# Three modulation steps a unit in the first MLP's second half, and the gate multiplied into three weight tiles of the second MLP

## Chip, core and metric

The kernel runs on one core of a Trainium2 chip. The core has five engines that run side by side, each through its own instructions in order: TensorE (PE) for matmuls, VectorE (DVE), ScalarE (ACT), GpSimd (POOL), and SyncE (SP), which here only issues DMAs. Weights come from HBM by DMA. The metric is the device time of one execution in microseconds (us).

## What is computed

Two transformer layers with adaptive modulation over 256 latent tokens (t = 0, 1 of 128 tokens each) and, in the first layer only, 256 context tokens (t = 2, 3). Layer 0 mixes by retention, layer 1 by neighbourhood attention; each is followed by an MLP. The parts that matter here:

```python
mod = (silu_c @ ada_w[i] + ada_b[i])[:, None, :]
sh1, sc1, g1, sh2, sc2, g2 = jnp.split(mod, 6, axis=-1)
...
x = layer_norm(DN_ALPHA * x + g1 * y, ln_g[i, 0], ln_b[i, 0])
h = x * (1.0 + sc2) + sh2
x = layer_norm(DN_ALPHA * x + g2 * sq_relu_mlp(h, mlp_w1[i], mlp_w2[i]), ln_g[i, 1], ln_b[i, 1])
```

`sq_relu_mlp` is `square(relu(h @ w1)) @ w2` with 4096 hidden columns. The gate g2 is one number per output column, the same for all tokens, so `g2 * (r @ w2)` is `r @ (w2 * g2)`.

## The kernel before

**Precision.** Every float32 operand is split into a high half (`hi`, a rounded cast by ACT) and a low half (`lo = raw - hi`, by DVE), and each product is three matmuls (hi*hi, hi*lo, lo*hi; `mm3`). So each weight tile goes through a fixed path: a DMA of 512 KB into a `raw` buffer (SP), a cast to `hi` (ACT), a subtraction to `lo` (DVE), then matmuls. `raw` has four buffers, `hi` and `lo` five each. `specs` lists all weight tiles in the order of use; `take` and `fetch` (L250 on) bring them in, `take` up to five ahead.

**Modulation as background work.** The products with `ada_w` that layer 1 needs are made bit by bit beside the matmuls. `bg(n)` (L556) does n steps; a step loads one 512 KB slice of `ada_w` (`rawa`, into the same four raw buffers and by the same SP queue) and has DVE weigh the slice before it into an accumulator (`acc<-rawa`). Each eight slices end in a fold (`red<-acc`) and some small work. There are 89 steps (`bg_max`); 41 are done before the first MLP, 16 in the second layer of its first half.

**First MLP (layer 0).** The hidden columns are done in two halves (`hf`). A half has eight units of the first layer (two weight tiles, 48 matmuls of 512 columns, then a squared relu into `hid` by ACT and DVE), and then the second layer over two halves of the output columns, each with eight weight tiles (24 matmuls each) into four PSUM banks. In the half with hf = 1, `bg(2 + fp % 2)` (L1332) does two and three steps by turns after each unit, 20 in all, and `bg()` (L1357) one after each of the next twelve weight tiles; with that the 89 are done. The last four weight tiles of the last half are held (`held = take(4)`): they are multiplied token tile by token tile, so that the normalization of one tile can run beside the matmuls of the next, and all four are needed within the first token tile's 24 matmuls.

**Second MLP (layer 1).** Only latent tokens. Its second layer has 16 units u of 256 weight rows, each in two halves of the output columns; `parts` holds four PSUM accumulators (token tile t, half). The last three units (HELD = 13 on) are held and done in the order (t 0, half 0), (t 0, half 1), (t 1, half 0), (t 1, half 1), the last of these in two quarters of the columns that have PSUM banks of their own. `settle` multiplies an accumulator by the gate (`gated`, DVE, out of PSUM) and adds it to the residual R; `settle_quarter` does it for a quarter; `stat` and `moments` make the mean and variance, `last_norm` the output. From the held units on, PE, ACT, DVE and POOL keep the order of the program text. Nearly all instructions are recorded in one helper (`InOrder`, L84), so the profile's rows all carry L84, and tiles tell them apart.

In the order of the held part, `settle(1, 1)`, for the finished units of (t 1, half 1), stands between the two halves of token tile 0.

Of the kernel before, what the change touches and what calls it, by code (L numbers as in the profile page):

```python
# [17 lines left out]
P = 128  # L18
# [86 lines left out]
def kernel(  # L105
# [23 lines left out]
    pe, act, dve, pool, sp = (  # L129
        InOrder(tc, getattr(nc, e), e in PIN)  # L130
        for e in ("tensor", "scalar", "vector", "gpsimd", "sync")
    )
# [23 lines left out]
    def bank(s="ps"):  # L156
        return psp.tile([P, 512], F32, tag="ps", name=nm(s))
# [5 lines left out]
    def scr(s, dt=F32):  # L163
        return scp.tile([P, 512], dt, tag="scr", name=nm(s))
# [18 lines left out]
    specs = []  # L183
# [54 lines left out]
    def spec_w2(u, half):  # L238
        w_rows(mlp_w2[1], u * 256, 256, half * 512, 512)


    scratch_units = set()
    for u in range(16):
        for half in range(2):
            if (u, half) == (10, 0):
                scratch_units.add(len(specs))
                spec_w2(13, 0)
            if (u, half) != (13, 0):
                spec_w2(u, half)

    units = []
# [3 lines left out]
    def fetch(n, in_scratch=False, at=None):  # L255

        for src, k, ncol in specs[len(units) : len(units) + max(n, 0)]:
            raw = rawp.tile([P, k, ncol], F32, tag="raw", name=nm("raw"))
            sp.dma_start(out=raw[:], in_=src.rearrange("(k p) n -> p k n", p=P))
            if in_scratch or len(units) in scratch_units:  # L260
                hi, lo = Rows([scr("hi", F32R) for _ in range(k)]), Rows([scr("lo", F32R) for _ in range(k)])
                for i in range(k):
                    act.copy(out=hi[:, i, :], in_=raw[:, i, :])
                    pending.append((lo[:, i, :], raw[:, i, :], hi[:, i, :]))
                units.append((hi, lo))
                continue
            if at is None:
                hi = hip.tile([P, k, ncol], F32R, tag="hi", name=nm("hi"))
                lo = lop.tile([P, k, ncol], F32R, tag="lo", name=nm("lo"))
            else:  # L270
                both = slot(at, [P, 2, k, ncol], F32R, "hilo")
                hi, lo = both[:, 0], both[:, 1]
            act.copy(out=hi[:], in_=raw[:])
            pending.append((lo[:], raw[:], hi[:]))
            units.append((hi, lo))
# [99 lines left out]
    R = [RR[t // 2][:, t % 2, :] for t in range(4)]  # L375
# [180 lines left out]
    def bg(n=1):  # L556
        for _ in range(n):
            if bg_done[0] < bg_max[0]:
                flush()
                bg_done[0] += 1  # L560
                next(bgs, None)
# [5 lines left out]
    def load_gate(l, w, nt=2, eng=nc.scalar):  # L567
        G = cpool.tile([P, 2, D], F32, tag="G", name=nm("G"))
        gt = grow[l, w]
        for t in range(nt):  # L570
            eng.dma_start(out=G[:, t, :], in_=gt[t : t + 1, :].broadcast_to([P, D]))
        return G
# [83 lines left out]
    def stat(t, half):  # L656
        if half == 0:
            stats[t] = smp.tile([P, 2, 6], F32, tag="st", name=nm("st"))
        dve.bn_stats(out=stats[t][:, half, :], in_=R[t][:, half * 512 : (half + 1) * 512])
# [212 lines left out]
    def part_v(k, a, b):  # L872
# [8 lines left out]
        out=lgn[:, 0], in_=ret_decay[0].rearrange("(o d) h -> o (d h)", o=1).broadcast_to([P, 8])  # L881
# [118 lines left out]
    for h in range(RH):  # L1000
# [9 lines left out]
        else:  # L1010
# [15 lines left out]
            for u in range(4):  # L1026
                ((wh, wl),) = take(1)
                for t in range(4):
                    for kk in range(2):
                        k = 2 * u + kk  # L1030
# [72 lines left out]
        for t in range(4):  # L1103
            po = bank("po")
            scs = list(range(4)) if t < 2 else [2, 3]
            for i, sc in enumerate(scs):
# [9 lines left out]
                out=on, in0=po[:], scalar1=mv[:, 0:1], scalar2=r[:], op0=ALU.subtract, op1=ALU.mult  # L1116
# [51 lines left out]
        else:  # L1168
# [35 lines left out]
            tmp = proj(1, 1)  # L1204
# [10 lines left out]
            tmp = proj(2, 1)  # L1215
# [54 lines left out]

    G2 = None
    for hf in range(2):
# [46 lines left out]
        for fp in range(len(hid), 8):  # L1319
            ht = hslot(fp)  # L1320
            pb = [bank("p1") for _ in range(2)]
            us = take(2)
            mm1(us, ALL, pb)
            pe.on = False
            dve.on = hf == 0
            evac1(pb, ALL, ht)
            if hf == 0 and fp < 6:
                residual(fp - 2, xns[fp - 2], gb, dve)
            dve.on = False
            hid.append(ht)  # L1330
            if hf:
                bg(2 + fp % 2)  # L1332
            if hf == 0 and fp < 6:
                for q in range(16 * (fp - 2), 16 * (fp - 1)):
                    shifted_biases(q)
        if G2 is None:
            G2 = load_gate(0, 1)
        for half in range(2):
# [19 lines left out]
            if not last:  # L1358
                for t in range(4):
                    accumulate(pb[t], t, half, G2)  # L1360
                continue
            bg_until(89)
            held = take(4)
# [14 lines left out]
            def settle(t):  # L1378

                add_to(t, 1, gated(pb[t], t, 1, G2), dve)  # L1380
                stat(t, 1)
                return moments(t)
# [336 lines left out]
    p2 = turn(2)  # L1719
# [183 lines left out]
    ps = bank("pnw")  # L1903
# [93 lines left out]
    ps = [wo_last(1, 1, cols) for cols in HALVES]  # L1997
# [58 lines left out]


    G2 = load_gate(1, 1, 1)
    HS1 = [N_Q, N_V, N_B, N_P0, N_P1, N_OH, N_OL, N_K1]
    hid = [ht]  # L2060
    for f4 in range(1, 8):
# [22 lines left out]

    FULL = slice(0, 512)
    parts = {(t, half): [(bank("p2"), FULL)] for t in range(2) for half in range(2)}
    HELD = 13

    def mm2b(t, half, u, un, only=None):
        wh, wl = un  # L2090
        for i, (ps, cols) in enumerate(parts[t, half]):
            if only in (None, i):
                for kk in range(2):
                    k = 2 * u + kk
                    ht = hid[k // 4]
                    mm3(
                        ps[:, cols],
                        (ht[:, k % 4, 0, tsl(t)], ht[:, k % 4, 1, tsl(t)]),
                        (wh[:, kk, cols], wl[:, kk, cols]),
                        k == 0 or (len(parts[t, half]) > 1 and k == 2 * HELD),  # L2100
                        k == 31 or (t == half == 1 and k == 2 * HELD - 1),
                    )

    held = {}
    for u in range(HELD):
        if u == 10:
# [13 lines left out]
    def quarter(q):  # L2120
        return slice(256 * q, 256 * q + 256)
# [3 lines left out]

    def settle_quarter(q):
        ps = parts[1, q // 2][q % 2][0][:, quarter(q % 2)]
        tmp = scr("acc")
        dve.tensor_mul(out=tmp[:, :256], in0=ps, in1=G2[:, 0, quarter(q)])
        dve.tensor_add(out=R[1][:, quarter(q)], in0=R[1][:, quarter(q)], in1=tmp[:, :256])  # L2130
        stat_quarter(q)

    def stat_quarter(q):
# [14 lines left out]
        if a:  # L2148
            (sp, act)[half].dma_start(out=out[0, tsl(t), sl], in_=xn)

    for half in range(2):
        for u in range(13, 16):
            mm2b(0, half, u, held[u, half])
        if half == 0:
            settle(1, 1)
            parts[1, 1] = [(bank("p2"), slice(256 * q, 256 * q + 256)) for q in range(2)]
        settle(0, half)
        stat(0, half)
    m0 = moments(0)
    for half in range(2):  # L2160
        last_norm(0, 0, half, *m0)
# [51 lines left out]
```

## Time and profile before

| | us |
|---|---|
| median of 3 runs | 1177.96 (1176.31 to 1180.05) |
| the profiled execution | 1176.32 |
| its span, first to last instruction | 1174.4 |
| PE busy | 1161.8 |
| DVE busy | 848.4 |
| ACT busy | 481.1 |

Rows of the timeline give start, duration, engine, operation, output<-inputs and shape, and in brackets how long the engine had been idle and what ended it. "x2" puts equal neighbours in one row. Matmuls are pipelined, so a row's duration is longer than the distance to the next one's start; a PE gap is read from start to start. An SP row gives the time at which a DMA was issued. The granted TensorE clock was 0.998 of full speed on average.

### The profile page before, as it was taken

How to read it: one execution, taken by the hardware profiler on the slowest of the kernel's cores; microseconds unless marked ns; L12 is line 12 of the kernel's file. 1: busy time of each engine (PE TensorE's matmuls, PEld its weight loads, DVE VectorE, ACT ScalarE, POOL GpSimd, SP SyncE). 2: the span in 40 equal slices, each digit the busy share in tenths (PEclk: the TensorE clock that was granted, in tenths of full speed). 3: DMA queues.
4: the chain of work that ended last, by engine and by line, in shares of the span. 5: the costliest groups of instructions: out<-in, count | busy, mean ns of one | idle time of the engine just before them, and what ended most of it. 6: DMA issues, size and time to landing. Idle time of an engine off the chain costs nothing.

```text
span 1174.4 us, 17544 instructions
## 1 busy us (share of the span) xinstructions
PE 1161.8 (99%) x6687; PEld 980.7 (84%) x6687; DVE 848.4 (72%) x1361; ACT 481.1 (41%) x819; POOL 235.1 (20%) x418
## 2 busy tenths in 40 slices
PE   9999999999999999999999999999999999999997
PEld 6788888888888889888888888879778878999886
DVE  3786687777898787757777675578577589877456
ACT  3643332222323246441212333137466666756341
POOL 0102001010220241770312001223443430000001
PEclk9999999999999999999999999999999999999999
DMA  9943552544355426756556665646344335766760
GB/s 275 277 130 105 162 187 96 156 153 144 112 178 177 140 65 220 181 113 215 177 184 198 211 200 179 197 157 202 81 136 144 107 113 160 214 206 205 237 215 36
DMA packets 140115, 195.10 MB, mean 166 GB/s; under 512 B 9936, under 2 KB 81136, under 8 KB 140032
## 3 DMA queue, kind: packets, MB, share of 16 engines
q1 hardware_dynamic: 131904, 182.03, 49.8%
q0 software_dynamic: 6976, 9.39, 3.8%
q10 hardware_dynamic: 1152, 2.56, 0.7%
q8 instruction: 52, 0.85, 0.3%
q14 instruction: 31, 0.25, 0.1%
HBM read 189.12 MB, written 5.75 MB: 166 GB/s over the span
## 4 chain that ended last, share of the span: by engine, by line
PE 74%; DMA 12%; DVE 8%; issue 3%; ACT 2%; POOL 0%; DVEq 0%; ACTq 0%
PE p L84 23%; DMA rawa<-in_ada_w_dram 11%; PE pq L84 8%; PE pv L84 8%; PE pw L84 7%; PE pg L84 7%; PE pn L84 4%; DVE acc L84 4%; PE pnv L84 4%; PE po L84 3%; DVE lo L84 3%; PE pnw L84 1%; PE ppt L84 1%; PE pS L84 1%; PE pav L84 1%
## 5 line engine op out<-in xcount | busy, mean ns | idle before, releaser
L84 ACT CAST hi<-raw 128x1024 fp32r<-128x1024 f32 (+2 forms) x228 | 231.9, 1032 | 306.7 <-PE p L84 114.2
L84 DVE TENSOR_TENSOR lo<-raw,hi 128x1024 fp32r<-128x1024 f32 (+2 forms) x228 | 272.6, 1210 | 101.3 <-ACT hi L84 101.1
L84 PE MATMUL p<-hi,hid 128*128 128x512 f32 (+1 forms) x780 | 238.2, 386 | 0.0
L84 PEld LDWEIGHTS p<-hi,hid 128*128 128x128 f32 x780 | 145.7, 188 | 29.3
L84 PE MATMUL p<-hTl,hi 128*128 128x256 f32 (+1 forms) x512 | 165.9, 326 | 0.0
L84 PE MATMUL p<-hTh,lo 128*128 128x256 f32 (+1 forms) x512 | 165.9, 326 | 0.0
L84 PE MATMUL p<-hTh,hi 128*128 128x256 f32 (+1 forms) x512 | 162.6, 327 | 0.0
L84 PE MATMUL p<-lo,hid 128*128 128x512 f32 (+1 forms) x390 | 150.8, 387 | 2.1 <-DVE lo L84 2.1
L84 DVE SCALAR_TENSOR_TENSOR acc<-rawa,scol,acc 128x1024 f32<-128x1024 f32 x56 | 74.4, 1341 | 65.1 <-DMA rawa<-in_ada_w_dram 65.1
L84 PEld LDWEIGHTS p<-hTh,lo 128*128 128x128 f32 x512 | 96.3, 188 | 8.8
L84 PEld LDWEIGHTS p<-hTl,hi 128*128 128x128 f32 x512 | 96.4, 188 | 8.7
L84 PEld LDWEIGHTS p<-hTh,hi 128*128 128x128 f32 x512 | 94.3, 188 | 8.7
L84 PEld LDWEIGHTS p<-lo,hid 128*128 128x128 f32 x390 | 73.3, 188 | 17.9 <-DVE lo L84 3.2
L84 DVE SCALAR_TENSOR_TENSOR strips<-rawa,scol,strips 128x512 f32<-128x512 f32 x112 | 78.6, 764 | 0.0
L84 ACT CAST hid<-r 128x256 fp32r<-128x256 f32 (+1 forms) x64 | 31.9, 500 | 112.4 <-DVE r L84 112.3
L84 POOL TENSOR_TENSOR rstd<-rstd,misc 128x1 f32<-128x1 f32 x28 | 19.1, 684 | 216.5 <-DVE rstd L84 215.5
L84 ACT ACTIVATE s<-s,mn 128x512 f32<-128x512 f32 x64 | 45.5, 713 | 21.6 <-DVE mn L84 21.6
L84 PE MATMUL pw<-hi,oh 128*128 128x512 f32 x128 | 50.8, 397 | 0.0
L84 PE MATMUL pg<-hi,hTh 128*128 128x512 f32 x128 | 50.6, 395 | 0.0
L84 PE MATMUL pw<-hi,ol 128*128 128x512 f32 x128 | 50.0, 390 | 0.0
L84 PE MATMUL pg<-hi,hTl 128*128 128x512 f32 x128 | 49.9, 390 | 0.0
L84 PE MATMUL pw<-lo,oh 128*128 128x512 f32 x128 | 49.8, 389 | 0.0
(241 smaller groups left out, 2275.2 us busy)
## 6 DMA issues: line engine op xcount, KB each, us to landing
raw<-in_mlp_w_dram SPq DMA_DIRECT2D x128, 512.0 KB, 4.5
rawa<-in_ada_w_dram SPq DMA_DIRECT2D x80, 512.0 KB, 3.9
raw<-in_ret_w_in_dram SPq DMA_DIRECT2D x42, 512.0 KB, 4.0
raw<-in_nat_w_in_dram SPq DMA_DIRECT2D x24, 512.0 KB, 4.1
rawq<-in_ada_w_dram SPq DMA_DIRECT2D x16, 512.0 KB, 6.0
raw<-in_ret_w_o_dram SPq DMA_DIRECT2D x16, 512.0 KB, 3.5
bias<-rpb_rows POOLq DMA_DIRECT2D x32, 128.0 KB, 2.9
raw<-in_nat_w_o_dram SPq DMA_DIRECT2D x8, 512.0 KB, 3.7
```

The lines of the kernel that those rows point to most:

```text
L84: r = f(*args, **kwargs)
```

## The change

Three edits. First, `bg(2 + fp % 2)` becomes `bg(3)`: 24 steps instead of 20 in the eight units, so that the 89 are done four steps earlier and the last half of the second layer has none. Second, the tiles of units 13 to 15, half 1, of the second MLP's second layer are multiplied by the gate in place, between their DMA and their cast (three products of 128x2x512 by DVE). Third, what these tiles give for half 1 goes to banks of its own (one for token tile 0, two quarters for token tile 1, as before), is added to R without a further product, and the accumulators of units 0 to 12 of half 1 are settled with the gate for both token tiles after `settle(0, 0)`.

```diff
--- before.py
+++ after.py
@@ -239,13 +239,16 @@
         w_rows(mlp_w2[1], u * 256, 256, half * 512, 512)
 
 
-    scratch_units = set()
+    HELD = 13
+    scratch_units, scaled_units, scale_row = set(), set(), [None]
     for u in range(16):
         for half in range(2):
             if (u, half) == (10, 0):
                 scratch_units.add(len(specs))
                 spec_w2(13, 0)
             if (u, half) != (13, 0):
+                if half == 1 and u >= HELD:
+                    scaled_units.add(len(specs))
                 spec_w2(u, half)
 
     units = []
@@ -257,6 +260,10 @@
         for src, k, ncol in specs[len(units) : len(units) + max(n, 0)]:
             raw = rawp.tile([P, k, ncol], F32, tag="raw", name=nm("raw"))
             sp.dma_start(out=raw[:], in_=src.rearrange("(k p) n -> p k n", p=P))
+            if len(units) in scaled_units:
+                dve.tensor_mul(
+                    out=raw[:], in0=raw[:], in1=scale_row[0].unsqueeze(1).broadcast_to([P, k, ncol])
+                )
             if in_scratch or len(units) in scratch_units:
                 hi, lo = Rows([scr("hi", F32R) for _ in range(k)]), Rows([scr("lo", F32R) for _ in range(k)])
                 for i in range(k):
@@ -1329,7 +1336,7 @@
             dve.on = False
             hid.append(ht)
             if hf:
-                bg(2 + fp % 2)
+                bg(3)
             if hf == 0 and fp < 6:
                 for q in range(16 * (fp - 2), 16 * (fp - 1)):
                     shifted_biases(q)
@@ -2056,6 +2063,7 @@
 
 
     G2 = load_gate(1, 1, 1)
+    scale_row[0] = G2[:, 0, 512:1024]
     HS1 = [N_Q, N_V, N_B, N_P0, N_P1, N_OH, N_OL, N_K1]
     hid = [ht]
     for f4 in range(1, 8):
@@ -2084,7 +2092,6 @@
 
     FULL = slice(0, 512)
     parts = {(t, half): [(bank("p2"), FULL)] for t in range(2) for half in range(2)}
-    HELD = 13
 
     def mm2b(t, half, u, un, only=None):
         wh, wl = un
@@ -2097,8 +2104,8 @@
                         ps[:, cols],
                         (ht[:, k % 4, 0, tsl(t)], ht[:, k % 4, 1, tsl(t)]),
                         (wh[:, kk, cols], wl[:, kk, cols]),
-                        k == 0 or (len(parts[t, half]) > 1 and k == 2 * HELD),
-                        k == 31 or (t == half == 1 and k == 2 * HELD - 1),
+                        k == 0 or (half == 1 and k == 2 * HELD),
+                        k == 31 or (half == 1 and k == 2 * HELD - 1),
                     )
 
     held = {}
@@ -2125,9 +2132,7 @@
 
     def settle_quarter(q):
         ps = parts[1, q // 2][q % 2][0][:, quarter(q % 2)]
-        tmp = scr("acc")
-        dve.tensor_mul(out=tmp[:, :256], in0=ps, in1=G2[:, 0, quarter(q)])
-        dve.tensor_add(out=R[1][:, quarter(q)], in0=R[1][:, quarter(q)], in1=tmp[:, :256])
+        dve.tensor_add(out=R[1][:, quarter(q)], in0=R[1][:, quarter(q)], in1=ps)
         stat_quarter(q)
 
     def stat_quarter(q):
@@ -2148,14 +2153,18 @@
         if a:
             (sp, act)[half].dma_start(out=out[0, tsl(t), sl], in_=xn)
 
-    for half in range(2):
-        for u in range(13, 16):
-            mm2b(0, half, u, held[u, half])
-        if half == 0:
-            settle(1, 1)
-            parts[1, 1] = [(bank("p2"), slice(256 * q, 256 * q + 256)) for q in range(2)]
-        settle(0, half)
-        stat(0, half)
+    for u in range(HELD, 16):
+        mm2b(0, 0, u, held[u, 0])
+    settle(0, 0)
+    stat(0, 0)
+    for t in range(2):
+        settle(t, 1)
+    parts[0, 1] = [(bank("p2"), FULL)]
+    parts[1, 1] = [(bank("p2"), slice(256 * q, 256 * q + 256)) for q in range(2)]
+    for u in range(HELD, 16):
+        mm2b(0, 1, u, held[u, 1])
+    dve.tensor_add(out=R[0][:, FULL.stop :], in0=R[0][:, FULL.stop :], in1=parts[0, 1][0][0][:])
+    stat(0, 1)
     m0 = moments(0)
     for half in range(2):
         last_norm(0, 0, half, *m0)
```

PE's order of matmuls is the same in both programs. DVE's isn't. Here is a unit of two steps of the first MLP before, from its first slice on (`acc<-rawa` weighs a slice, `r` and `hid` make the hidden tile of the unit that PE has just done, `lo` belongs to the next units' weights):

```order
L84 SCALAR_TENSOR_TENSOR acc_5635<-rawa_5713,scol,acc_5635 128x1024
L84 TENSOR_TENSOR hid_5467<-r_5535,hid_5467 128x512
L84 SCALAR_TENSOR_TENSOR acc_5635<-rawa_5716,scol,acc_5635 128x1024
L84 SCALAR_TENSOR_TENSOR r_5609<-p_854_5547,r_5609 128x512
L84 TENSOR_TENSOR hid_5546<-r_5609,hid_5546 128x512
L84 TENSOR_TENSOR lo_5646<-raw_5643,hi_5645 128x1024
L84 TENSOR_TENSOR lo_5652<-raw_5649,hi_5651 128x1024
```

and a unit of three steps in the changed program:

```order
L84 SCALAR_TENSOR_TENSOR acc_5562<-rawa_5719,scol,acc_5562 128x1024
L84 SCALAR_TENSOR_TENSOR acc_5562<-rawa_5722,scol,acc_5562 128x1024
L84 SCALAR_TENSOR_TENSOR r_5627<-p_859_5565,r_5627 128x512
L84 TENSOR_TENSOR hid_5564<-r_5627,hid_5564 128x512
L84 SCALAR_TENSOR_TENSOR acc_5562<-rawa_5725,scol,acc_5562 128x1024
L84 TENSOR_TENSOR lo_5652<-raw_5649,hi_5651 128x1024
L84 TENSOR_REDUCE red_5561<-acc_5562 128x32
L84 SCALAR_TENSOR_TENSOR r_5632<-p_860_5566,r_5632 128x512
L84 TENSOR_TENSOR lo_5658<-raw_5655,hi_5657 128x1024
```

There is a third weighing, and the first `lo` follows it at once; between the two `lo` stand a fold and the second `r`. On the SP queue the last weight tiles of that MLP's second layer stood before with slices between them (`raw<-in_mlp_w` are weights, `rawa` slices, `gb` the layer norm's rows):

```order
L84 DMA rawa_6259<-in_ada_w_dram 128x1024
L84 DMA raw_6278<-in_mlp_w_dram 128x2x512
L84 DMA rawa_6308<-in_ada_w_dram 128x1024
L84 DMA raw_6311<-in_mlp_w_dram 128x2x512
L84 DMA rawa_6341<-in_ada_w_dram 128x1024
L84 DMA raw_6344<-in_mlp_w_dram 128x2x512
L84 DMA rawa_6374<-in_ada_w_dram 128x1024
L84 DMA raw_6377<-in_mlp_w_dram 128x2x512
```

and stand now without:

```order
L84 DMA rawa_6238<-in_ada_w_dram 128x1024
L84 DMA raw_6241<-in_mlp_w_dram 128x2x512
L84 DMA raw_6289<-in_mlp_w_dram 128x2x512
L84 DMA gb_6415<-lns 128x1024 x2
L84 DMA raw_6319<-in_mlp_w_dram 128x2x512
L84 DMA raw_6349<-in_mlp_w_dram 128x2x512
L84 DMA raw_6379<-in_mlp_w_dram 128x2x512
```

`raw_6278` to `raw_6377` before and `raw_6289` to `raw_6379` now are the four held tiles. No slice is left among them. Last, DVE from the end of the second MLP's weights on, before (`acc<-p,G` is the product with the gate, `p_1643` to `p_1646` the accumulators of (0, 0), (0, 1), (1, 0), (1, 1)):

```order
L84 TENSOR_TENSOR lo_10892<-raw_10889,hi_10891 128x1024
L84 TENSOR_TENSOR acc_10914<-p_1646_10401,G_9373 128x512
L84 TENSOR_TENSOR R_104<-R_104,acc_10914 128x512
L84 TENSOR_TENSOR acc_10919<-p_1643_10398,G_9373 128x512
L84 TENSOR_TENSOR R_104<-R_104,acc_10919 128x512
L84 BN_STATS st_10922<-R_104 128x6
L84 TENSOR_TENSOR acc_10942<-p_1644_10399,G_9373 128x512
L84 TENSOR_TENSOR R_104<-R_104,acc_10942 128x512
L84 BN_STATS st_10922<-R_104 128x6
```

and now:

```order
L84 TENSOR_TENSOR lo_10895<-raw_10891,hi_10894 128x1024
L84 TENSOR_TENSOR acc_10917<-p_1643_10398,G_9373 128x512
L84 TENSOR_TENSOR R_104<-R_104,acc_10917 128x512
L84 BN_STATS st_10920<-R_104 128x6
L84 TENSOR_TENSOR acc_10922<-p_1644_10399,G_9373 128x512
L84 TENSOR_TENSOR R_104<-R_104,acc_10922 128x512
L84 TENSOR_TENSOR acc_10925<-p_1646_10401,G_9373 128x512
L84 TENSOR_TENSOR R_104<-R_104,acc_10925 128x512
L84 TENSOR_TENSOR R_104<-R_104,p_1742_10928 128x512
L84 BN_STATS st_10920<-R_104 128x6
```

Settling of (1, 1) has moved behind those of (0, 0) and (0, 1), and the new bank `p_1742` is added without a product.

## The prediction

> **What bounds the kernel now.** I read the page's busy table first, then what PE waited for, then PE's own rows where it waited.
>
> ```profile
> PE 1161.8 (99%) x6687; PEld 980.7 (84%) x6687; DVE 848.4 (72%) x1361; ACT 481.1 (41%) x819; POOL 235.1 (20%) x418
> ```
> ```profile
> PE p L84 <- DVE lo L84: 2.1, 2, 1.7
> ```
> ```profile
> 765.92 0.61 PE L84 MATMUL p<-hi,hid 128*128 128x512 f32 x2
> 768.23 0.50 PE L84 MATMUL p<-lo,hid 128*128 128x512 f32 x1 [1.70 <-DVE lo L84]
> ...
> 769.27 0.63 PE L84 MATMUL p<-hi,hid 128*128 128x512 f32 x2
> 770.33 0.50 PE L84 MATMUL p<-lo,hid 128*128 128x512 f32 x1 [0.43 <-DVE lo L84]
> ```
> PE is the bound: 99% busy. A 512-wide matmul starts every 0.227 us, and between the start-up and the tail there is one place where it stands still, the four held units at the end of the first MLP. There the pair begun at 765.92 should be followed at 766.37, and is at 768.23 (1.86 lost); 769.27 should be followed at 769.72, and is at 770.33 (0.61); the first matmul after each gap costs 0.11 more. Together **2.7 us**. That, and the tail behind PE's last matmul, is all the change can win. What it can lose is PE's cover elsewhere, so the question is how far ahead of PE the weight stream runs.
>
> **The stream in the first MLP's second half.** PE takes 87.04 us for its eight units, 10.88 each:
>
> ```profile
> 612.38 0.39 PE L84 MATMUL p<-hTh,hi 128*128 128x512 f32 x1
> ...
> 699.42 0.39 PE L84 MATMUL p<-hi,hid 128*128 128x512 f32 x1
> ```
> Unit n starts at 612.38 + 10.88n, and first needs the low half of its second weight tile 14 matmuls in, 3.17 later: 648.2, 659.1, 670.0, 680.8, 691.7 for units 3 to 7. The low halves come in pairs (second tile of unit n, first tile of unit n+1); in DVE's rows the first of each pair is:
>
> ```profile
> 643.16 1.23 DVE L84 TENSOR_TENSOR lo<-raw,hi 128x1024 fp32r<-128x1024 f32 x1
> ...
> 655.37 2.35 DVE L84 TENSOR_TENSOR lo<-raw,hi 128x1024 fp32r<-128x1024 f32 x2
> ...
> 666.26 2.36 DVE L84 TENSOR_TENSOR lo<-raw,hi 128x1024 fp32r<-128x1024 f32 x2 [0.27 <-ACT hi L84]
> ...
> 677.84 1.22 DVE L84 TENSOR_TENSOR lo<-raw,hi 128x1024 fp32r<-128x1024 f32 x1
> ...
> 689.91 2.36 DVE L84 TENSOR_TENSOR lo<-raw,hi 128x1024 fp32r<-128x1024 f32 x2 [0.26 <-ACT hi L84]
> ```
> Each is done 1.22 after its start, so the lead over PE is 3.8, 2.5, 2.5, 1.8 and 0.6 us. **The stream is slower than PE already** (11.7 us a unit against 10.88), and lives on a lead that is used up just when the half ends. The added steps fall into this stretch. The windows view (stretch, then each engine's busy time and count, the granted clock, DMA share, GB/s) shows that DMA is not full there, and that the clock stays full in the gap at the hold:
>
> ```profile
> 612.00:699.00 87.00, 87.00 (x386) 72.03 (x385) 60.79 (x70) 26.57 (x39) 11.88 (x20) 1.00 0.65 201
> ...
> 765.00:771.00 6.00, 3.87 (x16) 2.57 (x15) 5.80 (x11) 2.10 (x2) 0.51 (x1) 1.00 0.77 237
> ```
> With four raw buffers the stream is a chain of waits. In a unit of three steps: the low half frees a buffer, slice 1 is issued into it, lands, is weighed; that frees the buffer of slice 3, which lands and is weighed, and then the next low half runs. Slice 2 and both weight tiles run beside that.
>
> ```profile
> 631.95 1.48 SPq L84 DMA_DIRECT2D rawa<-in_ada_w_dram  x2
> ...
> 667.52 5.24 SPq L84 DMA_DIRECT2D rawa<-in_ada_w_dram  x3
> ...
> 679.08 2.63 SPq L84 DMA_DIRECT2D rawa<-in_ada_w_dram  x2
> ...
> 702.97 0.37 SPq L84 DMA_DIRECT2D rawa<-in_ada_w_dram  x1
> ```
> ```profile
> 637.51 1.29 DVE L84 SCALAR_TENSOR_TENSOR acc<-rawa,scol,acc 128x1024 f32<-128x1024 f32 x1 [3.85 <-DMA rawa<-in_ada_w_dram]
> ...
> 648.04 0.75 DVE L84 TENSOR_SCALAR acc<-rawa,scol 128x1024 f32<-128x1024 f32 x1 [0.94 <-DMA rawa<-in_ada_w_dram]
> ...
> 653.56 1.28 DVE L84 SCALAR_TENSOR_TENSOR acc<-rawa,scol,acc 128x1024 f32<-128x1024 f32 x1 [0.89 <-DMA rawa<-in_ada_w_dram]
> ...
> 671.08 1.28 DVE L84 SCALAR_TENSOR_TENSOR acc<-rawa,scol,acc 128x1024 f32<-128x1024 f32 x1 [1.85 <-DMA rawa<-in_ada_w_dram]
> ...
> 676.03 1.28 DVE L84 SCALAR_TENSOR_TENSOR acc<-rawa,scol,acc 128x1024 f32<-128x1024 f32 x1 [0.76 <-DMA rawa<-in_ada_w_dram]
> ...
> 685.10 0.75 DVE L84 TENSOR_SCALAR acc<-rawa,scol 128x1024 f32<-128x1024 f32 x1 [3.18 <-DMA rawa<-in_ada_w_dram]
> ...
> 707.55 1.29 DVE L84 SCALAR_TENSOR_TENSOR acc<-rawa,scol,acc 128x1024 f32<-128x1024 f32 x1 [2.87 <-DMA rawa<-in_ada_w_dram]
> ```
> Slice 1, from issue to weighing, takes two lengths. Behind a unit of two steps 3.56 (667.52 to 671.08; four such, mean 3.84). Behind a unit of three steps, whose last weight tile was issued only 1.7 us earlier, 5.56, 4.32, 6.02 and 4.58 (first 631.95 to 637.51, longest 679.08 to 685.10, last 702.97 to 707.55): mean **5.12**. Slice 3 takes 3.67 from the end of the first weighing (672.36 to 676.03), at most 4.77 (648.79 to 653.56), mean of four 4.05.
>
> **The change part by part.**
>
> *Three steps a unit.* It adds four steps to this half and takes the last four out of the last half of the second layer, whose rawa issues no longer stand between the held weights. The 2.7 us there go: after the change a held tile waits only for a hi buffer, that of the last one is released a unit before the hold begins (5.44 us), and a cast and a low half follow in 1.05 + 1.23. The price is in the first layer. Every unit now follows a unit of three steps, so every slice 1 is a slow one (its neighbour is issued 1.2 us ahead, not 1.7). By the new DVE order the low half stands right behind the third weighing. A unit of the stream: 5.12 + 1.28 + 4.05 + 1.20 (weighing, start to start) + 1.22 (low half) = **12.87 us**. (For the unit 667 to 679 the same sum, with 3.56, 3.67 and the hid that stood between, 0.61, gives 11.54; the rows give 11.58.)
>
> Where it starts: the third slice of unit 0 can be issued once the weighing of 613.60 is done.
>
> ```profile
> 613.60 1.28 DVE L84 SCALAR_TENSOR_TENSOR acc<-rawa,scol,acc 128x1024 f32<-128x1024 f32 x1 [2.93 <-DMA rawa<-in_ada_w_dram]
> ...
> 619.00 1.28 DVE L84 TENSOR_TENSOR acc<-p,G 128x512 f32<-128x512 f32 x2
> ```
> 614.88 + 4.05, behind the first of these two products: weighed 619.65 to 620.93. Then twice a slow slice and a third one: 627.3, 632.7, 639.1, 643.1, and the low half of unit 3 at 645.5, 1.1 later than before, lead 2.7. From there 12.87 a unit: 658.4 (needed 659.1), 671.3 (1.3 late), 684.1 (needed 1.3 later by now: 2.0 late), 697.0 (2.0 late). **PE stands still for 5.3 us in units 5 to 7.** Each microsecond that PE is late is lead for the rest, so nothing is added in the second layer, where one slice a unit remains:
>
> ```profile
> 737.74 1.22 DVE L84 TENSOR_TENSOR lo<-raw,hi 128x1024 fp32r<-128x1024 f32 x1
> ...
> 753.57 1.22 DVE L84 TENSOR_TENSOR lo<-raw,hi 128x1024 fp32r<-128x1024 f32 x1
> ```
> Four low halves, 5.28 us apart, against PE's 24 x 0.227 = 5.44.
>
> *Gate in the weights.* Three products of 128x1024 join DVE in the second MLP. No row shows one with a broadcast operand; of this size a step takes 0.75 (685.10, one tensor in) to 1.29 (707.55, two), the low half with its two inputs 1.23, which I take: 3.7 in all. They cannot gain, since nothing waits less for them. What covers them: the last tile is cast at 1150.34 and its low half is done at 1152.66; PE needs it third in the batch of held units that follows 1154.42, 12 matmuls (2.7) in, near 1157.1.
>
> ```profile
> 1150.34 1.05 ACT L84 CAST hi<-raw 128x1024 fp32r<-128x1024 f32 x1 [1.67 <-PE p L84]
> ```
> ```profile
> 1151.43 1.23 DVE L84 TENSOR_TENSOR lo<-raw,hi 128x1024 fp32r<-128x1024 f32 x1 [1.50 <-ACT hi L84]
> 1152.57 0.69 DVE L84 TENSOR_TENSOR acc<-p,G 128x512 f32<-128x512 f32 x1
> ...
> 1154.42 0.69 DVE L84 TENSOR_TENSOR acc<-p,G 128x512 f32<-128x512 f32 x1 [0.44 <-PE p L84]
> ...
> 1158.50 0.69 DVE L84 TENSOR_TENSOR acc<-p,G 128x512 f32<-128x512 f32 x1 [1.93 <-PE p L84]
> ...
> 1165.97 0.42 DVE L84 TENSOR_TENSOR R<-R,acc 128x256 f32<-128x256 f32 x1
> 1166.43 0.43 DVE L84 BATCH_NORM_STATS2 st<-R 128x6 f32<-128x256 f32 x1
> 1166.89 0.42 DVE L84 TENSOR_TENSOR acc<-p,G 128x256 f32<-128x256 f32 x1
> ```
> ```profile
> 1166.58 0.28 PE L84 MATMUL p<-hi,hid 128*128 128x256 f32 x1
> ```
> Even all three in a row would leave 0.7 us. Taken: 0; without that cover, what exceeds 4.4 us would show on PE.
>
> *The tail.* The product of 1166.89 goes, with its gap 0.46 (likewise the one of the quarter before). PE's last matmul ends at 1166.86, exactly where DVE comes free now, so the new sum cannot start earlier: of the two products only one shows. Against it, settling the finished accumulators of half 1 is moved behind 1154.42: 5.1 us of DVE work from there to 1159.5, so the sum over the new bank starts 1.0 late and ends 0.25 later than now. DVE has 0.46 of slack from the other product, which takes that. Gain **0.5**; bounds 0 (the delay grows) and 0.9 (both products).
>
> Sum: 5.3 - 2.7 - 0.5 = **+2.1 us** on the profiled execution, 1176.32 to 1178.4. The runs shown have a median 1.64 above it; on that median 1180.1.
>
> **Rivals.**
> *No new stall.* If slice 1 lands as behind units of two steps, 3.84, a stream unit is 11.59 and the last low half 0.2 late: 0.2 - 2.7 - 0.5 = -3.0, 1175.0. For it: DMA share 0.65, 201 GB/s. Against: the four with a close neighbour (4.32 to 6.02) lie above the four without (3.56 to 4.44) but for one pair. The Trainium skill, "DMA: Bandwidth & Descriptors", Specifications, gives a core about 358 GB/s from HBM; by that estimate five tiles of 512 KB need 7.3 us of a unit's 10.88, and the third step would be free. The trace differs: its units of five tiles took 11.5 to 12.8.
> *A slower stream (slower than before by over 0.3%).* With 6.02 and 4.77, the longest rows, a stream unit is 14.49 and the stall 11.8: +8.6, 1186.6. It decides from 13.2 us a unit, where the stall passes 6.7; half way, 13.6, gives +5.0, 1183.0. For it: more tiles in flight in every unit. By the Trainium skill, "TensorE: Matmul & The Clock Gate", Part 1, a window of 3.4 us without work halves PE's clock, which would add some 1.7 us a time, an estimate; the 1.86 us gap here left the granted clock at 1.00.
> *Not what it says.* The hold at 766 stalls as before, because the low halves wait there for something other than slices, and the first layer pays too: +4.8, 1182.8. Against: the only work between those low halves is rawa's.
>
> **How the numbers follow.** Forecast 0.53, no new stall 0.22, slower stream 0.22, not what it says 0.03. 0.3% is 3.5 us, about what measurement tells from no change. The first rival's -3.0 lies inside; the runs spread by +-1.9, so a third of it may read faster: 0.07. Slower 0.22 (slower stream) and a little of the third: 0.23. Same 0.70. The range goes from 1174.6 (no new stall, less 0.4) to 1183.5 (half-way stream); beyond it are the far end of the second rival and the lucky runs, under 0.2.
>
> **What would show it.** PE waiting for lo between 665 and 698, in units 5 to 7, about 2 us each; pairs of low halves about 12.9 apart there; no wait at the held units; from PE's last matmul to the end 0.5 less. I am wrong if the pairs come 11.6 apart (no stall) or over 13.2, or if the hold still waits.

## The result, and the profile after

Over 22 runs each, the median is 1178.81 us after the change and 1175.35 before; the ratio is **1.0031, 95% interval [1.0021, 1.0042]**. The change costs 3.5 us. (One of the 22 runs after, at 1695 us and a granted clock of 0.64, is in a slow state and is left out of the ratio.) The profiled executions stand closer: span 1176.5 after, 1174.4 before, so +2.1, the figure that was forecast. The page's busy table and what PE waited for, after:

```profile
PE 1162.7 (99%) x6687; PEld 980.6 (83%) x6687; DVE 852.7 (72%) x1363; ACT 480.9 (41%) x819; POOL 236.2 (20%) x418
```
```profile
PE p L84 <- DVE lo L84: 4.1, 3, 1.6
```

Three waits in place of two. The table alone does not say where they are; PE's own rows in the timeline do (start, duration, ..., in brackets the idle time and what ended it):

```profile
612.53 0.39 PE L84 MATMUL p<-hTh,hi 128*128 128x512 f32 x1
...
669.91 0.39 PE L84 MATMUL p<-hTl,hi 128*128 128x512 f32 x1
671.59 0.50 PE L84 MATMUL p<-hTh,lo 128*128 128x512 f32 x1 [1.30 <-DVE lo L84]
...
682.42 0.39 PE L84 MATMUL p<-hTl,hi 128*128 128x512 f32 x1
684.39 0.50 PE L84 MATMUL p<-hTh,lo 128*128 128x512 f32 x1 [1.58 <-DVE lo L84]
...
695.22 0.39 PE L84 MATMUL p<-hTl,hi 128*128 128x512 f32 x1
696.88 0.50 PE L84 MATMUL p<-hTh,lo 128*128 128x512 f32 x1 [1.27 <-DVE lo L84]
...
704.72 0.39 PE L84 MATMUL p<-hi,hid 128*128 128x512 f32 x1
```

From start to start less 0.227, the gaps are 1.45, 1.74 and 1.43, with 0.11 after each: 4.95 us, in units 5, 6 and 7 of the first MLP's second half. The half takes 704.72 - 612.53 = 92.19 where it took 87.04. The low halves that PE waits for, in DVE's rows, with the two weighings that stand in the chain between the first two of them:

```profile
645.21 1.22 DVE L84 TENSOR_TENSOR lo<-raw,hi 128x1024 fp32r<-128x1024 f32 x1
...
651.38 2.67 DVE L84 SCALAR_TENSOR_TENSOR acc<-rawa,scol,acc 128x1024 f32<-128x1024 f32 x2 [1.19 <-DMA rawa<-in_ada_w_dram]
656.54 1.28 DVE L84 SCALAR_TENSOR_TENSOR acc<-rawa,scol,acc 128x1024 f32<-128x1024 f32 x1 [0.51 <-DMA rawa<-in_ada_w_dram]
657.74 2.35 DVE L84 TENSOR_TENSOR lo<-raw,hi 128x1024 fp32r<-128x1024 f32 x2
...
670.32 1.22 DVE L84 TENSOR_TENSOR lo<-raw,hi 128x1024 fp32r<-128x1024 f32 x1
...
683.12 2.35 DVE L84 TENSOR_TENSOR lo<-raw,hi 128x1024 fp32r<-128x1024 f32 x2
...
695.60 2.35 DVE L84 TENSOR_TENSOR lo<-raw,hi 128x1024 fp32r<-128x1024 f32 x2
```
```profile
646.46 0.37 SPq L84 DMA_DIRECT2D rawa<-in_ada_w_dram  x1
...
652.70 0.37 SPq L84 DMA_DIRECT2D rawa<-in_ada_w_dram  x1
```

Read them as a chain: the low half ends at 646.43, a slice is issued at 646.46 and weighed from 651.38 to 652.67, the next is issued at 652.70 and weighed from 656.54, and behind it comes the next low half. The firsts of the pairs end at 646.43, 658.96, 671.54, 684.34 and 696.82: 12.60 us apart in the mean, against PE's 10.88.

The windows view (stretch, busy time and count of PE, PEld, DVE, ACT, POOL, clock, DMA share, GB/s) shows the same half, and the hold, where nothing stands still now:

```profile
612.00:700.00 88.00, 83.85 (x368) 68.36 (x367) 63.99 (x71) 26.44 (x38) 13.46 (x22) 1.00 0.67 209
...
765.00:771.00 6.00, 6.00 (x28) 4.97 (x27) 2.02 (x2) 1.62 (x2) 0.00 (x0) 1.00 0.81 246
```

The tail of DVE's rows, with PE's last matmul:

```profile
1165.91 1.41 DVE L84 TENSOR_TENSOR R<-R,acc 128x512 f32<-128x512 f32 x1
...
1169.50 0.42 DVE L84 TENSOR_TENSOR R<-R,p 128x256 f32<-128x256 f32 x1 [0.60 <-PE p L84]
```
```profile
1169.18 0.28 PE L84 MATMUL p<-hi,hid 128*128 128x256 f32 x1
```

PE's last matmul ends at 1169.46 and the sum starts 0.04 later, after 0.60 us of idle time: DVE waits for PE, not the other way round. From there to the end of the span it is 7.05 us, and was 7.52 (1166.86 to 1174.37): 0.5 less.

### The profile page after: what moved, and what is told of

Its sections match the earlier page's. It is cut to its first block, busy times and chain, and to the rows that moved or that the text cites. A ratio compares the mean times of both kernels' runs of the same rounds, so it can differ in the third digit from the quotient of the medians.

```text
span 1176.5 us, 17536 instructions
## 1 busy us (share of the span) xinstructions
PE 1162.7 (99%) x6687; PEld 980.6 (83%) x6687; DVE 852.7 (72%) x1363; ACT 480.9 (41%) x819; POOL 236.2 (20%) x418
## 4 chain that ended last, share of the span: by engine, by line
PE 80%; DMA 9%; DVE 6%; issue 2%; SPq 1%; ACT 1%; POOL 0%; ACTq 0%; DVEq 0%
PE p L84 29%; PE pw L84 7%; PE pg L84 7%; DMA rawa<-in_ada_w_dram 7%; PE pq L84 7%; PE pv L84 7%; PE pn L84 5%; PE pnv L84 4%; PE po L84 3%; DVE acc L84 3%; DVE lo L84 2%; PE ppt L84 2%; PE pnw L84 1%; PE pS L84 1%; PE pav L84 1%
## 5 line engine op out<-in xcount | busy, mean ns | idle before, releaser
L84 DVE TENSOR_TENSOR hid<-r,hid 128x256 fp32r<-128x256 f32 (+1 forms) x64 | 34.5, 540 | 26.4 <-ACT hid L84 26.4
L84 PE MATMUL pq<-hTh,hi 128*128 128x512 f32 x128 | 49.3, 395 | 0.8 <-ACT hTh L84 0.4
```

Of the source, the lines that this page charges most:

```text
L84: r = f(*args, **kwargs)
```

## The experiments

The theory that all of them test: the time is made of three terms, the stall in units 5 to 7 (+5.3), the gap at the held units (-2.7) and the tail (-0.5), and the first comes from slices and weights waiting for each other's four raw buffers. The main rivals: the transfers cannot come faster, or a cost sits where no wait shows.

### The parts apart

Tail edit alone, and three steps a unit alone (the first is the changed kernel with this line, the second the kernel before with its opposite):

```diff
-                bg(3)
+                bg(2 + fp % 2)
```

> The tail edit without the three steps a unit. Theory (terms of the prediction add up): no wait of PE for lo in units 5 to 7 of the first MLP's second half, the 2.7 us at the four held units back, the tail 0.5 us shorter: 0.5 us less than before, ratio 0.9996. Rival (the change costs more than its three terms, and the rest sits in the tail edit, for instance in the three products): no difference or slower than before, ratio 1.000 to 1.002.

> Three steps a unit without the tail edit. Theory: PE waits for lo three times in units 5 to 7, together some 5.1 us, nothing at the held units (2.7 won): +2.4 us, ratio 1.0020, tail as before. Rival (the runs show 3.5 us where the profile shows 2.1, and the rest lies in this part): +3.5 to +4 us, ratio 1.003 or more.

tail_alone: 1175.03 against 1175.46, ratio 0.9995 [0.9977, 1.0014]; in the profile 7.06 us from PE's last matmul to the end, no wait in the units, and one gap at the held units, of 0.7 us instead of 2.7:

```profile
766.69 0.63 PE L84 MATMUL p<-hi,hid 128*128 128x512 f32 x2
767.72 0.50 PE L84 MATMUL p<-lo,hid 128*128 128x512 f32 x1 [0.39 <-DVE lo L84]
```

The time alone cannot tell the two expectations apart, 0.9996 and 1.000 to 1.002: both lie in the interval.

steps_alone: 1179.51, ratio 1.0033 [1.0017, 1.0049]; the half takes 92.96 us (+5.9), nothing waits at the held units, the tail is as before (7.51). PE waits in units 5 and 6 only, 2.0 us each, and not three times. What it loses besides is clock: after the second wait the granted clock is 0.52 for 3 us, and matmuls start 0.43 us apart in place of 0.227.

```profile
682.67 0.39 PE L84 MATMUL p<-hTl,hi 128*128 128x512 f32 x1
684.85 0.58 PE L84 MATMUL p<-hTh,lo 128*128 128x512 f32 x1 [1.79 <-DVE lo L84]
685.24 0.63 PE L84 MATMUL p<-hTh,hi 128*128 128x512 f32 x1
685.66 0.63 PE L84 MATMUL p<-hTl,hi 128*128 128x512 f32 x1
```
```profile
685.00:688.00 3.00, 3.00 (x8) 2.34 (x9) 2.23 (x3) 1.11 (x2) 0.00 (x0) 0.52 0.84 228
```

That is 1.6 us over the eight matmuls from 685.24 on. In this time the stream catches up: the low half for unit 7 is ready 0.2 us before PE needs it. So the slow stretch stands in place of the third wait.

The parts add up, -0.4 and +4.1 against +3.5 for both. All of the loss is in the three steps. But the loss is nearer to the rival's 3.5 to 4 than to 2.4: the half lost somewhat more here, and the gap that goes was not always 2.7.

tail_alone without its three products on the weights:

```diff
-            if len(units) in scaled_units:
+            if False:
```

> tail_alone without the three products on the weights (the gate is left out for the last three units of the second half). Theory: the products stand beside idle time of DVE, so the time is that of tail_alone within what can be measured, and the tail from PE's last matmul to the end 7.0 us in both. Rival (the products hold up DVE or the raw buffers): 1 to 3.7 us less than tail_alone. It also gives one more sample of the gap at the held units, which the theory puts between 0.7 and 2.7.

1175.15, ratio 0.9998 [0.9981, 1.0015], the tail 7.05. The products show no cost; the interval alone would leave room for some 2 us, but in the changed kernel's rows each of the three stands behind 2.2 to 3.3 us of waiting for its own transfer, and PE waits for nothing there. The first and the last:

```profile
1138.38 1.23 DVE L84 TENSOR_TENSOR raw<-raw,G 128x1024 f32<-128x1024 f32 x1 [2.16 <-DMA raw<-in_mlp_w_dram]
...
1151.03 1.23 DVE L84 TENSOR_TENSOR raw<-raw,G 128x1024 f32<-128x1024 f32 x1 [3.25 <-DMA raw<-in_mlp_w_dram]
```

### What makes the stall: buffers, transfers or their number

The hidden tiles of units 6 and 7 have places of 8 KB that lie free until those units. In own_buffers the slices loaded in units 0 to 4 go there:

```diff
+    own, own_tile = [None], [None]
...
-        raw = rawp.tile([P, 2, 512], F32, tag="raw", name=nm("rawa"))
+        if own[0] is None:
+            raw = rawp.tile([P, 2, 512], F32, tag="raw", name=nm("rawa"))
+        else:
+            i = own[0]
+            own[0] += 1
+            if i % 2 == 0:
+                own_tile[0] = slot((S_VH, S_GS)[i // 2 % 2], [P, 4, 512], F32, "rawo")
+            raw = own_tile[0][:, 2 * (i % 2) : 2 * (i % 2) + 2, :]
...
+                if fp == 0:
+                    own[0] = 0
+                if fp == 5:
+                    own[0] = None
                 bg(3)
```

> The changed kernel, with the modulation slices that are loaded in units 0 to 4 put into two free 8 KB places (those of the hidden tiles of units 6 and 7) in place of the four raw buffers; same number of transfers, same order on every engine. Theory (the stream is a chain of waits on four shared buffers): the low halves come earlier than PE needs them in all units, no wait of PE for lo between 612 and 700, none at the held units: 87.0 us for the half, 3.2 us less than before, ratio 0.9973. Rival (the transfers themselves don't come faster than five of 512 KB in 12.6 us, or the weighings on DVE set the pace): the pairs of low halves stay 12.5 us apart, the stalls stay near 5 us, ratio 1.002 to 1.003.

1172.59, ratio **0.9984 [0.9970, 0.9997]**. PE waits for no low half, neither in the units nor at the hold. Its low halves for units 3, 4 and 7 come at

```profile
639.10 1.22 DVE L84 TENSOR_TENSOR lo<-raw,hi 128x1024 fp32r<-128x1024 f32 x1
...
650.99 1.21 DVE L84 TENSOR_TENSOR lo<-raw,hi 128x1024 fp32r<-128x1024 f32 x1
...
684.61 2.35 DVE L84 TENSOR_TENSOR lo<-raw,hi 128x1024 fp32r<-128x1024 f32 x2
```

and the windows row of the half shows 238 GB/s where the changed kernel has 209:

```profile
612.00:700.00 88.00, 88.00 (x390) 72.87 (x389) 68.47 (x81) 30.16 (x44) 17.52 (x32) 1.00 0.73 238
```

So the transfers can come faster, and DVE can weigh three slices a unit; waiting for the four shared buffers makes the stall. The transfers did not get quicker one by one (the page's DMA issues, median us from issue to landing in the last column; rawo are the slices with places of their own):

```profile
rawo<-in_ada_w_dram SPq DMA_DIRECT2D x15, 512.0 KB, 5.0
```

The changed kernel's slices in the same stretch, 612 to 700 us, took 4.8 in the median.

Then a higher dose, four steps a unit, with the shared buffers (four_steps) and with the free places (four_steps_own):

```diff
-                bg(3)
+                bg(4)
```

> Four steps a unit (all 32 in the eight units), four shared raw buffers. Theory (chain of waits): the fourth slice waits for the second one's weighing, which adds about one weighing (1.28) to a unit of the stream: 14.1 us a unit in place of 12.6, 3.3 over PE's 10.88, first late at unit 3 by some 2 us, 13 to 16 us of PE waiting for lo in units 3 to 7, none at the held units: +10 to +13 us, ratio 1.009 to 1.011. Rival (the fourth slice is hidden beside the third): 12.6 us a unit, +3 to +5.

> Four steps a unit, the slices of units 0 to 4 in the two free places. Six transfers of 512 KB a unit are 289 GB/s. Theory (the waits on the four buffers make the stall, not what the transfers can deliver; with five of them in flight the run own_buffers shows 9.56 us for the last to land, about 275 to 330 GB/s): no wait of PE for lo until unit 5, at most 2 us behind it: -3.2 to -1 us against before, ratio 0.997 to 0.999. Rival (delivery becomes the limit at six tiles a unit): 5 us or more of waiting for lo in units 3 to 7, ratio over 1.002.

four_steps_own did as expected: 1172.76, ratio 0.9988 [0.9976, 0.9999], no wait. **four_steps did not**: 1173.94, ratio 0.9993 [0.9980, 1.0007], where +10 to +13 us were expected. PE waits 0.6 and 0.2 us:

```profile
692.11 0.50 PE L84 MATMUL p<-hTh,lo 128*128 128x512 f32 x1 [0.46 <-DVE lo L84]
```

Six transfers a unit on the same four buffers stall less than five. So it isn't the number of slices, and the theory that each slice more adds its weighing to the chain falls. The rows tell how the chain differs:

```profile
678.00 1.29 DVE L84 SCALAR_TENSOR_TENSOR acc<-rawa,scol,acc 128x1024 f32<-128x1024 f32 x1 [1.64 <-DMA rawa<-in_ada_w_dram]
...
683.27 1.28 DVE L84 SCALAR_TENSOR_TENSOR acc<-rawa,scol,acc 128x1024 f32<-128x1024 f32 x1
...
689.61 1.28 DVE L84 SCALAR_TENSOR_TENSOR acc<-rawa,scol,acc 128x1024 f32<-128x1024 f32 x1 [0.51 <-DMA rawa<-in_ada_w_dram]
690.82 1.24 DVE L84 TENSOR_TENSOR lo<-raw,hi 128x1024 fp32r<-128x1024 f32 x1
```
```profile
679.32 1.48 SPq L84 DMA_DIRECT2D rawa<-in_ada_w_dram  x2
...
684.58 6.68 SPq L84 DMA_DIRECT2D rawa<-in_ada_w_dram  x3
```

A slice is issued at 679.32, when the weighing of 678.00 has ended, weighed from 683.27 to 684.55, and the next is issued at 684.58 and weighed at 689.61. Weighing releases slice and slice weighing; the low half at 690.82 hangs at the end of this chain, but is no link of it. In the changed kernel it is a link: 646.43 releases the slice of 646.46. So which release a transfer waits for follows from the order in which the buffers are handed on, and these rows show another order with six tiles a unit than with five.

If so, the order alone should cure it, with three steps and four buffers. interleaved writes the same work as weight tile, step, weight tile, step, matmuls, step:

```diff
-            us = take(2)
+            if hf:
+                us = take(2, 4)
+                bg()
+                take(0, 3)
+                bg()
+            else:
+                us = take(2)
...
-                bg(3)
+                bg(1)
```

> The changed kernel with the same three steps a unit and four shared raw buffers, but written weight tile, step, weight tile, step, unit's matmuls, step, so that the transfers stand W s W s s in place of W W s s s. Theory (not the number of transfers sets the stall, but which release each waits for: a transfer gets the buffer that came free three releases before; in the changed kernel one slice waits for a low half, the next for that slice's weighing, and the low half stands behind the second: two landings one after the other in each unit, 12.6 us; here the slice that a low half releases is followed on DVE by slices that were issued before it, so one landing a unit stands on the chain): pairs of low halves at most 11.5 us apart, waits for lo in units 5 to 7 under 1.5 us in all, none at the held units: -3.2 to -1.5 us against before, ratio 0.997 to 0.999. Rival (five transfers, or three weighings and two low halves, on four buffers take 12.5 us in any order): 4 to 6 us of waiting, ratio 1.002 to 1.004.

1172.79 against 1173.38 in the same session, ratio 0.9989 [0.9978, 0.9999]: no wait in the units, none at the hold.

```profile
642.18 1.22 DVE L84 TENSOR_TENSOR lo<-raw,hi 128x1024 fp32r<-128x1024 f32 x1
...
653.53 2.36 DVE L84 TENSOR_TENSOR lo<-raw,hi 128x1024 fp32r<-128x1024 f32 x2
664.89 1.22 DVE L84 TENSOR_TENSOR lo<-raw,hi 128x1024 fp32r<-128x1024 f32 x1
...
677.57 2.35 DVE L84 TENSOR_TENSOR lo<-raw,hi 128x1024 fp32r<-128x1024 f32 x2
689.83 2.35 DVE L84 TENSOR_TENSOR lo<-raw,hi 128x1024 fp32r<-128x1024 f32 x2
```

But the pairs were to be at most 11.5 us apart, and are 11.36, 11.36, 12.68 and 12.26. The stall is gone as much for the earlier start as for the shorter distance. And the edit moves the weighings on DVE along with the loads; no run moves one without the other. Two numbers decide it in every kernel of the table below: the lead of the first low half of unit 3 over PE (which needs it 35.82 us after the half's first matmul), and four times what the stream's unit exceeds PE's 10.88:

| kernel | lead at unit 3 | stream's unit, mean of 4 | lead - 4 x excess | PE late in the half |
|---|---|---|---|---|
| before | 3.8 | 11.69 | +0.6 | 0 |
| after | 1.9 | 12.60 | -5.0 | 5.1 |
| after_again (below) | 3.9 | 12.79 | -3.7 | 3.9 |
| steps_alone | 2.1 | 12.83 | -5.7 | 5.9, of it 1.6 at the lower clock |
| four_steps | 4.2 | 12.16 | -0.9 | 1.1 |
| interleaved | 4.6 | 11.92 | +0.5 | 0 |
| own_buffers | 8.3 | 11.38 | +6.3 | 0 |

### The gap at the held units

steps_behind_held was to place the last four steps behind the taking of the held weights (from tail_alone):

```diff
-            bg_until(89)
             held = take(4)
+            bg_until(89)
```

> The tail edit, two or three steps a unit as before, and the last four steps placed behind the taking of the four held weight units. Theory (at the hold a low half is late only because the slices' transfers stand between the held weights): no wait at the held units, no stall in units 5 to 7: 3.2 us less than before, ratio 0.9973. Rival (the slices then hold up what stands behind them on DVE: the statistics, the gated sums and the gate columns of the last layer): a new wait of PE of 2 to 6 us between 766 and 800, ratio 0.999 to 1.003.

It moved nothing: all 89 steps were done by then, as the four stand in the half's first four units, between the transfers of the held tiles. So it is tail_alone a second time: 1175.26, ratio 1.0003 [0.9988, 1.0017], and a gap of 2.0 us where tail_alone had 0.7. slices_behind_held moves those four steps in truth (from tail_alone, too):

```diff
-                bg()
+                if not last:
+                    bg()
...
-            bg_until(89)
             held = take(4)
+            bg_until(89)
```

> The tail edit, two or three steps a unit as before, and all four steps of the last half's first four units placed behind the taking of the held units. (steps_behind_held moved nothing: its four steps had been done already in those units, so it is tail_alone a second time, and its gap at the held units of 2 us against 0.7 is the spread of one program.) Theory: no slice stands between the held weights, no wait of PE for lo at the held units, no stall in units 5 to 7: 0.7 to 2.7 us less than tail_alone, ratio to before 0.9965 to 0.9990. Rival (the slices hold up DVE's work behind the hold): a new wait of PE of 2 to 6 us between 770 and 800.

1181.58, ratio 1.0050 [1.0032, 1.0069]: the rival, by the same chain of waits. Now three weighings stand on DVE ahead of the last held low halves, and wait for slices that got their buffers late:

```profile
764.83 1.28 DVE L84 SCALAR_TENSOR_TENSOR acc<-rawa,scol,acc 128x1024 f32<-128x1024 f32 x1 [3.98 <-DMA rawa<-in_ada_w_dram]
...
769.81 1.28 DVE L84 SCALAR_TENSOR_TENSOR acc<-rawa,scol,acc 128x1024 f32<-128x1024 f32 x1 [2.56 <-DMA rawa<-in_ada_w_dram]
772.25 1.28 DVE L84 SCALAR_TENSOR_TENSOR acc<-rawa,scol,acc 128x1024 f32<-128x1024 f32 x1 [1.16 <-DMA rawa<-in_ada_w_dram]
773.45 1.22 DVE L84 TENSOR_TENSOR lo<-raw,hi 128x1024 fp32r<-128x1024 f32 x1
```
```profile
774.73 0.79 PE L84 MATMUL p<-lo,hid 128*128 128x512 f32 x1 [5.38 <-DVE lo L84]
```
```profile
774.00:780.00 6.00, 5.28 (x15) 4.25 (x16) 5.72 (x12) 0.00 (x0) 0.51 (x1) 0.62 0.86 274
```

The windows row behind the gap adds a price of its own: the granted clock is 0.62 in these 6 us, and only 15 matmuls run. A gap need not be that long: 2.0 us did the same in steps_alone, at 685 us. The other gaps, 1.86 us in the kernel before and 1.99 in after_again among them, left the clock at 1.00, so the length of a gap alone does not tell. The Trainium skill, "TensorE: Matmul & The Clock Gate", Part 1, has the clock halved after a window of 3.4 us without work. The 5.4 us here agree with it; the 2.0 us in steps_alone do not, and there the measurement decides.

steps_in_half_0 moves them the other way, into the first half of the second layer (from tail_alone):

```diff
-                bg()
+                bg(1 + hf * u % 2)
```

> The tail edit, two or three steps a unit as before, and the four steps of the last half moved one half earlier: in the first half of the second layer every second weight tile takes two steps in place of one. Theory (the gap at the held units is all that is to be won there, and is 0.7 to 2.7 us from execution to execution): no wait at the held units, no wait elsewhere, as PE stands 0 to 1 us behind the stream when that half begins and the weight tiles there come 5.4 us apart with one and a half slices each: 1.2 to 3.2 us less than before, ratio 0.9973 to 0.9990. Rival (five transfers in 10.88 us are too many there too, as in the units): PE waits for lo between 705 and 745 for 1 to 4 us, ratio 0.9995 to 1.002.

No wait for a low half in the units or in the second layer, and one of 0.2 us at the hold (at 766.20; 0.3 us lost with it), close to what the theory has. The time is not clear: median 1172.99 against 1173.37, ratio 1.0001 [0.9983, 1.0019].

### The same kernels again

> The changed kernel once more, beside the same runs of before as interleaved. Theory (the profiled execution of before, with 2.7 us at the held units, was one with a long gap there; the three others with the same order at that place show 0.7, 2.0 and 2.2): the stall in units 5 to 7 is 4.9 to 5.9 us again, so the difference of the medians is about 5.4 - 1.9 - 0.5 = +3.0 us, ratio 1.0026. Rival (a cost that no profile has shown): the medians differ by over 4 us, or PE waits at another place.

> The kernel before, once more, for the gap at its held units. Theory: between 0.7 and 2.7 us as in the four executions with the same order there, so that the 2.7 us of the profiled execution is at the long end. Rival (2.7 is typical of it): 2.5 us or more.

after_again: 1178.39, ratio 1.0045 [1.0030, 1.0060]; the half takes 90.96 us (+3.9), and PE waits nowhere else anew. Its profiled execution, 1176.96, is the fastest of its five runs, and holds less than their median: the rival's over 4 us came true in the runs, but no profile shows a place for it. before_again has **no gap at the held units at all** (the low half that PE waited for at 768.23 before is done 3 us ahead), against theory and rival. And yet its span is only 0.7 shorter than that of before, for a reason that no edit touches: PE's pace in the second MLP's first layer. The windows rows of 1010 to 1070 us, of before, before_again and after in this order, count PE's matmuls:

```profile
1010.00:1070.00 60.00, 60.00 (x531) 60.00 (x531) 47.62 (x74) 37.40 (x67) 0.00 (x0) 1.00 0.66 205
```
```profile
1010.00:1070.00 60.00, 60.00 (x512) 60.00 (x511) 47.73 (x71) 36.41 (x65) 0.00 (x0) 1.00 0.63 196
```
```profile
1010.00:1070.00 60.00, 60.00 (x532) 60.00 (x530) 47.99 (x74) 37.88 (x69) 0.00 (x0) 1.00 0.66 207
```

60 us hold 531, 512 and 532 matmuls: one in 0.113 us in before and after, one in 0.117 in before_again, with the granted clock at 1.00 in all three and PE busy throughout. steps_in_half_0 has the slow pace too (511); the other twelve of the fourteen profiled executions have 530 to 532. From the first matmul of the neighbourhood attention to the second MLP's second layer these two take 266.0 and 266.1 us, the twelve 263.0 to 263.5. So 2.8 us come and go with the execution.

## Why the prediction was right, and where it was off

**Three steps a unit: the stall.** Forecast 5.3 us in units 5 to 7, some 2 us each; the profile has 4.95 there, 1.4 to 1.7 each. Over the three executions with three steps in that order (after, after_again, steps_alone) the half took 5.1, 3.9 and 5.9 us more, mean 5.0. In the profile after, two errors of the working cancel: the lead at unit 3 was 1.9, not 2.7, and a unit of the stream 12.60, not 12.87. In the mean of the three executions, 2.6 and 12.74, both terms are close; but the leads spread from 1.9 to 3.9, so that one execution hits 5.3 within 0.4 is in part luck. In steps_alone there were two waits and a stretch of lower clock, not three waits. Slice 1 took 4.80 to 5.77 from issue to weighing in the profile after, 5.13 in the mean of seven, against the 5.12 taken; it was the rest of the chain that was shorter.

**The gap at the hold.** It goes, as forecast; nothing waits there in any kernel with three or four steps. The size is the term that was mis-sized: 2.7 was read from one execution. The others with that order at the hold have 0.7, 2.0, 2.2 and 0: the mean of five is 1.5. With it the sum is 5.0 - 1.5 - 0.5 = +3.0, against +3.5 measured, interval 2.5 to 4.9. The runs agree from the other side: the three kernels without any wait there or in the units (own_buffers, four_steps_own, interleaved) are 1.3 to 1.9 us faster than before by their ratios, which less 0.5 for the tail leaves 0.8 to 1.4 for the gap.

**Tail.** 0.5, in all executions with the edit but those of own_buffers and four_steps_own (7.15 there, 0.4). The products on the weights were taken at no cost; tail_no_products and the rows show none. The bound that was argued from, that the sum over the new bank might start late, did not come: DVE stood idle 0.60 us before the last quarter, although the add of 1165.91 took 1.41 us and not 0.69.

**The sum.** That the two profiled spans differ by the forecast +2.1 is partly luck: the three terms give 1.8 there, and the other 0.3 lies where no edit reaches, half of it ahead of this MLP half. The time came within 1.3 us, 1178.81 against the forecast 1180.1, by two errors against each other: the 1177.96 that it stood on, from three runs, is 1175.35 over 22, so the base was 2.6 too high and the difference 1.4 too low.

**Rivals.** "No new stall" and "not what it says" fell with the rows at 671 to 697 and 765 to 771. "A slower stream" did not decide: 12.60 to 12.83 us a unit, below its 13.2; the lowered clock that was named beside it came in steps_alone, after a gap of 2.0 us. One reading in the first rival was off: the three units of three steps that begin at 644.38, 667.49 and 691.14 in the rows before took 11.6 to 12.2, not up to 12.8. The chain of waits is shown in so far as the stall goes when slices get places of their own, and goes when the order is another. That each slice more lengthens it stood in no sum, but was believed until four_steps. Why the order cures it is read from the rows of these kernels; loads and weighings were always moved together.

**Open.** Of the +5.0 us of after_again's runs the profiles account for about 3, or for 4.5 if the runs of before in that session had no gap at the hold. The pace of PE in the second MLP moves an execution by nearly as much as the whole change does, and was not traced to a cause. How often it fell into the runs can't be seen without a profile; the 17 runs of before in the last session do lie in two groups, nine from 1172.3 to 1173.4 and eight from 1175.3 up, with none between, but a gap at the hold would part them in the same way.

## What to carry to other kernels

Where several kinds of tile share a pool of buffers, ask of each transfer which release it waits for: the order in which loads are written decides it, and writing the same loads in turn (weight, slice, weight, slice, slice), with the weighings moved along, took away a stall of 4 to 6 us. Four slices a unit stalled less than three. Before a gap in one profile is entered as a gain, look at a second execution: here it was anything from 0 to 2.7 us. Ask also what a wait does to PE's clock: after 2.0 us it fell by half once, and stayed full after others as long. Three versions beat the changed kernel, and the kernel before by 0.1 to 0.2%, with intervals that just leave out 1 and with the pace of PE above not under control: slices in places that lie idle, with three or with four steps a unit, and the interleaved order; the last needs no memory.

## What the hardware showed that was not expected

PE's pace without any wait: 128x256 matmuls every 0.113 us in twelve executions and every 0.117 us in two, at a granted clock of 1.00 in both. PE's clock: a gap of 2.0 us in steps_alone was followed by a granted clock of 0.52 from 685 to 688 us, one of 1.99 us in after_again by 1.00. And more transfers in flight give more bytes though each takes longer: in own_buffers six tiles issued from 609.8 to 613.0 us landed 3.64, 5.63, 6.94, 7.76, 8.74 and 9.56 us after their issue, and the half moved 238 GB/s in place of 209.
